# A change of engine for the duplicate of k's larger part in a three-block transformer kernel: VectorE in place of a GpSimd transfer

## The chip, the cores and the metric

The kernel runs on one core of a Trainium2 chip. The metric is the device time of one launch in microseconds; the time shown for a kernel is the median of several runs. TensorE (PE in the profile, PEld for its weight loads) multiplies matrices, VectorE (DVE) and ScalarE (ACT) work elementwise on up to 128 partitions, GpSimd (POOL) here clears tiles and issues some transfers, and SyncE (SP) issues the loads of weights. SBUF holds tiles of 128 partitions; PSUM takes TensorE's results.

## What is computed

The input x is 512 tokens of 1024 float32 values. Three blocks follow one another, each adding its result to x.

```python
def first_block(x, ...):            # block 1
    h = rms_norm(x, norm_mix)
    q, kc_raw, vc_raw, ks, vs, kw, vw, gates, hq, hf, hi, hg = split(h @ w_in)
    q, ks, kw = rms_norm of each head with its gain (ks, kw: 2 groups of 64)
    o_nsa  = gated sum of compressed, selected and windowed attention, 8 heads of 64
    o_hgrn = hgrn2_mixer(hq, hf, hi, hg)        # 4 heads of 128, chunks of 64
    x = x + concat(o_nsa, o_hgrn) @ w_out
    gate, up = split(rms_norm(x, norm_ffn) @ w_gate_up)
    return x + (silu(gate) * up) @ w_down

for l in range(2):                  # the two later layers, L0 and L1
    sb_q, sb_k, sb_v, df_q, df_k, df_v = split(rmsnorm(x) @ w_in[l])
    sb = stick_breaking_attention(sb_q, sb_k, sb_v)             # 8 heads of 64
    df = differential_attention(rope(df_q), rope(df_k), df_v)   # 4 x 2 heads of 64
    x = x + concat(sb, rmsnorm(df) * (1 - lambda_init)) @ w_o[l]
    x = x + square(relu(rmsnorm(x) @ w_ff1[l])) @ w_ff2[l]      # width 4096
return rmsnorm(x)
```

Everything has to hold float32 accuracy, while TensorE multiplies in a shorter format, fp32r. So an operand is split in two parts, a larger one (the value cast to fp32r) and a smaller one (the rest, also in fp32r), and a product is the sum of three or four products of parts.

## The kernel before

**Tiles.** Activations lie with features on the partitions and the 512 tokens along the free dimension. A dense product takes a weight tile, splits it (ScalarE casts the larger part, L284, VectorE subtracts, L285) and issues three matmuls for each 128 rows of the contraction (L289 to L291).

**The pairs for scores.** Heads have 64 features, so a tile of 128 partitions holds two heads. For a score product one matmul contracts over all 128 partitions: q is stacked as larger part on the head's own 64 partitions and smaller part on the other 64 (stacked_q, L315 to L323), and k must then have its larger part on both halves, so that one matmul gives both parts of q times the larger part of k. That is what stacked_k (L325 to L333) builds. For each of the two heads g, with r the head's own partitions and o the other 64, it clears the smaller part's tile on o (GpSimd, L329), casts the larger part on r (ScalarE, L330), subtracts for the smaller part on r (VectorE, L331) and duplicates the larger part on o (L332). A second matmul takes kl. The source t is a float32 tile of 128x512.

**Who calls it.** 18 calls, so 36 duplicates of 64x512: nk0 and nk1 in block 1 (L700; the normed tile nkn of L699), and in each later layer sk1, sk3, sk5, sk7 (L956, stick-breaking attention, from tile sb) and dk0 to dk3 (L979, differential attention, from the rotated tile rt). Their readers on TensorE are the scores s (L761, L762), z (L993, L994) and ds (L1078, L1079).

**What sets the order.** The program is written as streams that yield: dense products, HGRN heads and attention units. A driver interleaves them by a cost that each announces and by shares (ORDER1 and SHARES1 for block 1, ORDER2 and SHARES2 for a later layer). After that a scheduler places every instruction in its engine's queue by its own estimate of durations, within the limits of the buffer pools and PSUM banks (two banks of pool mm for dense products, three of pool s for scores and HGRN products). Each engine then works through its queue in that order and waits where an operand or a buffer isn't there. So a change of one instruction's engine can move others on every engine.

**HGRN head 3.** The change's surroundings in block 1 are the last of the HGRN heads. emit_hgrn makes x (hx, L426), hq (L431), hk (L435) and, after a table load and a logarithm on ScalarE, the running sum hc (L440). From hc, VectorE and ScalarE make qc, kc (L473 to L477) and the scaled qx, kx (L519 to L525), which the products hpo need (L528 to L534). Then come seven levels m = 64, 32, ..., 1: two or three VectorE operations make qr and ke (L488 to L504), four 64-column matmuls give hpl (L508), and VectorE merges the result into at (L510). The diagonal hpd (L544), the product hpv (L553 to L556) and the output follow. Dense work that can stand between: wvsw (values of the attention and gates), whg (gate of HGRN) and wout (the output product, the part over finished heads).

## Time and profile before

| | before |
|---|---|
| median of 3 runs | 2021.68 us |
| the runs | 2023.47, 2021.68, 2016.97 us |
| profiled execution: time | 2023.06 us |
| profiled execution: span from first to last instruction | 2021.3 us |
| mean granted TensorE clock | 0.995 |
| TensorE busy | 1981.6 us, 98% |
| VectorE busy | 1177.0 us, 58% |
| ScalarE busy | 878.0 us, 43% |
| GpSimd busy | 44.6 us, 2% |
| GpSimd's transfer queue | 2976 packets, 4.98 MB, 1.2% of 16 engines' span |

One execution is profiled; its rows are in microseconds from the span's start unless they say ns. A wait is the idle time of an engine ahead of an instruction, put down to what released it. An arrow a<-b names the tile written and the tiles read; L0 and L1 before a name are the later layers. An operation's duration in a timeline overlaps the next one's start a little, so a group of operations takes less than the sum of its durations; the chain of waits gives the time from one to the next.

### The profile page before, as it was taken

The page shows a single profiled execution, that of the slowest core. Times are in us where ns is not written, and L with a number is a line of the kernel's source. Part 1 is how long each engine was busy: PE and PEld are TensorE (multiplying, and loading weights), DVE is VectorE, ACT ScalarE, POOL GpSimd, SP SyncE. Part 2 cuts the span into 40 slices and gives each one's busy share as a digit, 9 for nine tenths or more (in the row PEclk, how much of TensorE's full clock was granted, in tenths as well). Part 3 has the DMA queues.
Part 4 walks back from the last instruction along what each step waited for, and adds up shares of the span by engine and source line. Part 5 has one row for each costly group of instructions (what it writes and reads, how often), then busy time and mean ns, then how long its engine had stood idle before and what let it go on. Part 6 is the DMA issues. An engine that isn't in the chain of part 4 may idle for free.

```text
span 2021.3 us, 25987 instructions
## 1 busy us (share of the span) xinstructions
PE 1981.6 (98%) x10269; PEld 1614.4 (80%) x10269; DVE 1177.0 (58%) x2032; ACT 878.0 (43%) x1420; POOL 44.6 (2%) x87
## 2 busy tenths in 40 slices
PE   8999999999999999999999999999999999999998
PEld 7888867788888878777788888887878788888887
DVE  7685876744444455657864444447466874444446
ACT  6643544522222235766542223335586653322223
POOL 0000000000000000000000000000000000000000
PEclk9999999999999999999999999999999999999999
DMA  5222200122222322212222222222212222232222
GB/s 185 69 68 89 61 13 31 63 94 94 94 94 97 98 89 84 73 48 76 68 94 94 94 94 94 95 99 89 80 51 69 64 83 94 98 100 94 94 94 73
DMA packets 50921, 168.64 MB, mean 83 GB/s; under 512 B 5808, under 2 KB 8240, under 8 KB 50800
## 3 DMA queue, kind: packets, MB, share of 16 engines
q1 hardware_dynamic: 47680, 161.93, 24.5%
q0 software_dynamic: 2976, 4.98, 1.2%
q8 instruction: 81, 1.33, 0.3%
q14 instruction: 40, 0.33, 0.1%
q10 hardware_dynamic: 144, 0.07, 0.0%
HBM read 160.14 MB, written 2.10 MB: 80 GB/s over the span
## 4 chain that ended last, share of the span: by engine, by line
PE 68%; issue 23%; DVE 4%; ACT 3%; DMA 2%; POOL 0%; SPq 0%; DVEq 0%; ACTq 0%; POOLq 0%
PE L1wf_p L291 5%; PE L1wf_p L289 5%; PE L1wf_p L290 5%; PE wgu_p L291 4%; PE wgu_p L289 4%; PE wgu_p L290 4%; PE wdn_p L289 2%; PE wdn_p L290 2%; PE wdn_p L291 2%; PE po L811 1%; PE hpl L508 1%; PE pt L792 1%; PE wout_p L289 1%; PE wout_p L290 1%; PE wout_p L291 1%
## 5 line engine op out<-in xcount | busy, mean ns | idle before, releaser
L284 ACT CAST L0wf_h<-L0wf_r 128x1024 fp32r<-128x1024 f32 x64 | 67.3, 1052 | 229.3 <-PE L0wf_p L291 224.8
L284 ACT CAST L1wf_h<-L1wf_r 128x1024 fp32r<-128x1024 f32 x60 | 63.1, 1051 | 221.0 <-PE L1wf_p L291 216.7
L291 PE MATMUL wgu_p<-h_l,wgu_h 128*128 128x512 f32 x328 | 128.8, 393 | 0.0
L289 PE MATMUL wgu_p<-h_h,wgu_h 128*128 128x512 f32 x328 | 128.7, 392 | 0.0
L290 PE MATMUL wgu_p<-h_h,wgu_l 128*128 128x512 f32 x328 | 128.6, 392 | 0.0
L284 ACT CAST wgu_h<-wgu_r 128x1024 fp32r<-128x1024 f32 x44 | 46.2, 1051 | 168.3 <-issue 65.1
L289 PE MATMUL L0wf_p<-L0u_h,L0wf_h 128*128 128x512 f32 x256 | 100.7, 393 | 0.0
L290 PE MATMUL L0wf_p<-L0u_h,L0wf_l 128*128 128x512 f32 x256 | 100.4, 392 | 0.0
L291 PE MATMUL L0wf_p<-L0u_l,L0wf_h 128*128 128x512 f32 x256 | 99.4, 393 | 0.0
L291 PE MATMUL L0wf_p<-L0m_l,L0wf_h 128*128 128x512 f32 x240 | 94.2, 393 | 0.0
L291 PE MATMUL L1wf_p<-L1m_l,L1wf_h 128*128 128x512 f32 x240 | 94.2, 393 | 0.0
L289 PE MATMUL L0wf_p<-L0m_h,L0wf_h 128*128 128x512 f32 x240 | 94.2, 392 | 0.0
L289 PE MATMUL L1wf_p<-L1m_h,L1wf_h 128*128 128x512 f32 x240 | 94.2, 392 | 0.0
L290 PE MATMUL L0wf_p<-L0m_h,L0wf_l 128*128 128x512 f32 x240 | 94.1, 392 | 0.0
L290 PE MATMUL L1wf_p<-L1m_h,L1wf_l 128*128 128x512 f32 x240 | 94.1, 392 | 0.0
L285 DVE TENSOR_TENSOR L0wf_l<-L0wf_r,L0wf_h 128x1024 fp32r<-128x1024 f32 x64 | 78.4, 1225 | 24.6 <-ACT L0wf_h L284 24.6
L289 PE MATMUL L1wf_p<-L1u_h,L1wf_h 128*128 128x512 f32 x224 | 88.1, 393 | 0.0
L290 PE MATMUL L1wf_p<-L1u_h,L1wf_l 128*128 128x512 f32 x224 | 87.9, 392 | 0.0
L285 DVE TENSOR_TENSOR L1wf_l<-L1wf_r,L1wf_h 128x1024 fp32r<-128x1024 f32 x60 | 73.5, 1225 | 23.2 <-ACT L1wf_h L284 23.2
L291 PE MATMUL L1wf_p<-L1u_l,L1wf_h 128*128 128x512 f32 x224 | 86.9, 393 | 0.0
L353 DVE TENSOR_TENSOR X<-X,L0wf_p 128x512 f32<-128x512 f32 x64 | 43.9, 687 | 67.2 <-PE L0wf_p L291 67.2
L353 DVE TENSOR_TENSOR X<-X,L1wf_p 128x512 f32<-128x512 f32 x56 | 38.5, 687 | 66.6 <-PE L1wf_p L291 66.6
(841 smaller groups left out, 5392.6 us busy)
## 6 DMA issues: line engine op xcount, KB each, us to landing
L0wf_r<-w_ff SPq DMA_DIRECT2D x64, 512.0 KB, 3.3
L1wf_r<-w_ff SPq DMA_DIRECT2D x60, 512.0 KB, 3.3
wgu_r<-w_gu SPq DMA_DIRECT2D x44, 512.0 KB, 3.3
wdn_r<-w_dn SPq DMA_DIRECT2D x22, 512.0 KB, 3.3
wns_r<-w_nsa SPq DMA_DIRECT2D x8, 512.0 KB, 3.6
wout_r<-w_out SPq DMA_DIRECT2D x8, 512.0 KB, 3.3
L0wsb_r<-w_sbqk SPq DMA_DIRECT2D x8, 512.0 KB, 3.3
L0wdf_r<-w_dfqk SPq DMA_DIRECT2D x8, 512.0 KB, 3.6
```

What stands on the lines that cost most here:

```text
L284: S.copy(hi[:, c], raw[:, c])
L285: V.tensor_tensor(lo[:, c], raw[:, c], _f(hi)[:, c], ALU.subtract)
L289: TE.matmul(ps, lh, rh, start=start, stop=False)
L290: TE.matmul(ps, ll, rh, start=False, stop=False)
L291: TE.matmul(ps, lh, rl, start=False, stop=stop)
L353: V.tensor_tensor(X[m], X[m], ps, ALU.add)
L508: TE.matmul(pl[:, b * 64 : (b + 1) * 64], ke[:, b * P : (b + 1) * P], qr[:, b * 64 : (b + 1) * 64], start=True, stop=True)
L792: TE.transpose(pt[:, o + j * P : o + (j + 1) * P], p[g][:, j * P : (j + 1) * P], ident)
L811: TE.matmul(po[g * 64 : (g + 1) * 64, 0:P], vsw[:, j, br * 128 + g * 64 : br * 128 + (g + 1) * 64], p[g][:, j * P : (j + 1) * P], start=Fa ...
```

## The change

L332, the last line of the loop in stacked_k, wrote the duplicate as a transfer from SBUF to SBUF, issued by GpSimd and reading ScalarE's result. It becomes a VectorE copy that reads the float32 source t on partitions r and writes fp32r on partitions o.

```diff
         for g, (r, o) in enumerate(((lower, upper), (upper, lower))):
             G.memset(_f(kl[o, g]), 0.0)
             S.copy(kh[r, g], t[r])
             V.tensor_tensor(kl[r, g], t[r], _f(kh[r, g]), ALU.subtract)
-            G.dma_start(kh[o, g], kh[r, g])
+            V.tensor_copy(kh[o, g], t[r])
         return kh, kl
```

All 36 transfers leave GpSimd's queue, and 36 copies (CAST in the order of instructions) come into VectorE's. The scheduler orders the engines anew. SyncE's queue changes in the place of one load only.

**VectorE, block 1, where the pairs nk0 and nk1 are made.** nkn are the normed keys of the selected and the windowed attention; hx and hq belong to HGRN head 3, wvsw_l is the smaller part of a weight. Before:

```order
L699 SCALAR_TENSOR_TENSOR nkn_1802<-nraw_712,qkg,nkpb_1793 128x512
L699 SCALAR_TENSOR_TENSOR nkn_1823<-nraw_712,qkg,nkpb_1814 128x512
L331 TENSOR_TENSOR nk0l<-nkn_1802,nk0h 64x512 x2
L331 TENSOR_TENSOR nk1l<-nkn_1823,nk1h 64x512 x2
L426 TENSOR_TENSOR hx_1888<-whqf_p_0_1863,st_rb 128x512
L285 TENSOR_TENSOR wvsw_l<-wvsw_r,wvsw_h 128x1120
L431 TENSOR_TENSOR hq_1892<-hx_1888,hsg_1890 128x512
L426 TENSOR_TENSOR hx_1925<-whqf_p_0_1900,st_rb 128x512
```

and after:

```order
L699 SCALAR_TENSOR_TENSOR nkn_1802<-nraw_712,qkg,nkpb_1793 128x512
L332 CAST nk0h<-nkn_1802 64x512 x2
L331 TENSOR_TENSOR nk0l<-nkn_1802,nk0h 64x512 x2
L699 SCALAR_TENSOR_TENSOR nkn_1823<-nraw_712,qkg,nkpb_1814 128x512
L426 TENSOR_TENSOR hx_1888<-whqf_p_0_1863,st_rb 128x512
L332 CAST nk1h<-nkn_1823 64x512
L285 TENSOR_TENSOR wvsw_l<-wvsw_r,wvsw_h 128x1120
L331 TENSOR_TENSOR nk1l<-nkn_1823,nk1h 64x512 x2
L332 CAST nk1h<-nkn_1823 64x512
L431 TENSOR_TENSOR hq_1892<-hx_1888,hsg_1890 128x512
L426 TENSOR_TENSOR hx_1925<-whqf_p_0_1900,st_rb 128x512
```

Four copies come in, and the second nkn and the nk1l pair move behind other work; hq and the second hx, with which HGRN head 3 begins, stand behind all of it.

**TensorE, block 1, the levels of HGRN head 3.** wvsw_p_2186 is the last token block of the values' product. Before, from hpl_64 on:

```order
L508 MATMUL hpl_64_1996<-qr_64_1994,kc_1951 128x64 x4
L290 MATMUL wvsw_p_2186<-wvsw_h,h_1_l 128x280
L291 MATMUL wvsw_p_2186<-wvsw_l,h_1_h 128x280
L289 MATMUL wvsw_p_2186<-wvsw_h,h_2_h 128x280
L290 MATMUL wvsw_p_2186<-wvsw_h,h_2_l 128x280
L291 MATMUL wvsw_p_2186<-wvsw_l,h_2_h 128x280
L289 MATMUL wvsw_p_2186<-wvsw_h,h_3_h 128x280
L508 MATMUL hpl_32_2009<-qr_32_2002,ke_32_2003 128x64 x4
L290 MATMUL wvsw_p_2186<-wvsw_h,h_3_l 128x280
L291 MATMUL wvsw_p_2186<-wvsw_l,h_3_h 128x280
L289 MATMUL wvsw_p_2186<-wvsw_h,h_4_h 128x280
L290 MATMUL wvsw_p_2186<-wvsw_h,h_4_l 128x280
```

and after, from the last hpo matmul on:

```order
L534 MATMUL hpo_1990<-qx_1978,kx_1979 128x256
L508 MATMUL hpl_64_1996<-qr_64_1994,kc_1951 128x64 x4
L508 MATMUL hpl_32_2009<-qr_32_2002,ke_32_2003 128x64 x4
L508 MATMUL hpl_16_2022<-qr_16_2015,ke_16_2016 128x64 x4
L508 MATMUL hpl_8_2074<-qr_8_2028,ke_8_2029 128x64 x4
L289 MATMUL wvsw_p_2186<-wvsw_h,h_0_h 128x280
L290 MATMUL wvsw_p_2186<-wvsw_h,h_0_l 128x280
L291 MATMUL wvsw_p_2186<-wvsw_l,h_0_h 128x280
```

The levels 64 to 8 stood among matmuls of wvsw and whg, and now stand together, with the wvsw block behind them.

**TensorE, a little later, at the first probabilities of the attention.** cpt are transposes of compressed-attention probabilities, pt those of the others, s scores, wout_p the output product. Before:

```order
L737 MATMUL cpt_2304<-packed,sc 128x128 x4
L737 MATMUL cpt_2309<-packed,sc 128x128 x4
L291 MATMUL wout_p_1_2662<-ho_m_l,wout_0_h 128x512
L761 MATMUL s_1_2291<-nk1h,nq_1252 128x256
L762 MATMUL s_1_2291<-nk1l,nq_1252 128x256
L763 LDWEIGHTS masks
L763 MATMUL s_1_2291<-masks 128x128
L761 MATMUL s_0_2328<-nk0h,nq_1252 128x256
L762 MATMUL s_0_2328<-nk0l,nq_1252 128x256
L763 LDWEIGHTS masks
L763 MATMUL s_0_2328<-masks 128x128
L792 MATMUL pt_0_2317<-packed,p_2277 128x128 x2
```

and after:

```order
L737 MATMUL cpt_2304<-packed,sc 128x128 x4
L737 MATMUL cpt_2309<-packed,sc 128x128 x4
L289 MATMUL wout_p_0_2542<-ho_m_h,wout_0_h 128x512
L290 MATMUL wout_p_0_2542<-ho_m_h,wout_0_l 128x512
L291 MATMUL wout_p_0_2542<-ho_m_l,wout_0_h 128x512
L289 MATMUL wout_p_0_2542<-ho_m_h,wout_0_h 128x512
L290 MATMUL wout_p_0_2542<-ho_m_h,wout_0_l 128x512
L291 MATMUL wout_p_0_2542<-ho_m_l,wout_0_h 128x512
L289 MATMUL wout_p_0_2542<-ho_m_h,wout_0_h 128x512
L290 MATMUL wout_p_0_2542<-ho_m_h,wout_0_l 128x512
L761 MATMUL s_1_2291<-nk1h,nq_1252 128x256
```

Eight of the 17 wout matmuls that stood ahead, among hpl_4 to hpv, now stand between cpt and the next scores, and the other nine a little further on.

**TensorE, first later layer, the first scores z of sk1.** L0wsb_p_0_6468 is a dense product of the stick-breaking projections. Before:

```order
L290 MATMUL L0wsb_p_0_6468<-L0h_h,L0wsb_1_l 128x512
L291 MATMUL L0wsb_p_0_6468<-L0h_l,L0wsb_1_h 128x512
L289 MATMUL L0wsb_p_0_6468<-L0h_h,L0wsb_1_h 128x512
L290 MATMUL L0wsb_p_0_6468<-L0h_h,L0wsb_1_l 128x512
L291 MATMUL L0wsb_p_0_6468<-L0h_l,L0wsb_1_h 128x512
L289 MATMUL L0wsb_p_0_6468<-L0h_h,L0wsb_1_h 128x512
L993 MATMUL L0z_6365<-L0sq_6318,L0sk1h 128x256
L994 MATMUL L0z_6365<-L0sq_6318,L0sk1l 128x256
L993 MATMUL L0z_6378<-L0sq_6318,L0sk1h 128x256
L994 MATMUL L0z_6378<-L0sq_6318,L0sk1l 128x256
```

and after:

```order
L290 MATMUL L0wsb_p_0_6468<-L0h_h,L0wsb_1_l 128x512
L291 MATMUL L0wsb_p_0_6468<-L0h_l,L0wsb_1_h 128x512
L289 MATMUL L0wsb_p_0_6468<-L0h_h,L0wsb_1_h 128x512
L993 MATMUL L0z_6365<-L0sq_6318,L0sk1h 128x256
L993 MATMUL L0z_6378<-L0sq_6318,L0sk1h 128x256
L290 MATMUL L0wsb_p_0_6468<-L0h_h,L0wsb_1_l 128x512
L291 MATMUL L0wsb_p_0_6468<-L0h_l,L0wsb_1_h 128x512
L289 MATMUL L0wsb_p_0_6468<-L0h_h,L0wsb_1_h 128x512
L290 MATMUL L0wsb_p_0_6468<-L0h_h,L0wsb_1_l 128x512
L291 MATMUL L0wsb_p_0_6468<-L0h_l,L0wsb_1_h 128x512
L994 MATMUL L0z_6365<-L0sq_6318,L0sk1l 128x256
L994 MATMUL L0z_6378<-L0sq_6318,L0sk1l 128x256
```

The first scores moved thirteen matmuls ahead, and those with the smaller part (sk1l) stand apart from them. On VectorE, the two copies for sk1h stand on either side of the split of svw_0 and the subtractions for sk1l; at sk7 the order is subtraction, copy, subtraction, copy where it was two subtractions.

## Rows read from the trace of the kernel before

**Rows 1.** The page's section 1: the span, then busy time, share of the span and number of instructions of each engine.
```profile
span 2021.3 us, 25987 instructions
...
PE 1981.6 (98%) x10269; PEld 1614.4 (80%) x10269; DVE 1177.0 (58%) x2032; ACT 878.0 (43%) x1420; POOL 44.6 (2%) x87
```

**Rows 2.** TensorE's waits over the whole span: its line and tile, what released it, us in total, times, longest.
```profile
PE L0z L993 <- DMA L0sk7h<-L0sk7h: 2.3, 1, 2.3
...
PE L1z L993 <- DMA L1sk1h<-L1sk1h: 1.5, 1, 1.5
...
PE hpo L528 <- DVE kx L521: 1.2, 2, 1.0
PE L1z L993 <- DMA L1sk7h<-L1sk7h: 1.1, 1, 1.1
PE L0z L993 <- DMA L0sk1h<-L0sk1h: 1.1, 1, 1.1
...
PE L0z L993 <- DMA L0sk3h<-L0sk3h: 0.8, 1, 0.8
...
PE L1z L993 <- DMA L1sk3h<-L1sk3h: 0.8, 1, 0.8
...
PE hpl L508 <- DVE qr L494: 0.4, 1, 0.4
```

**Rows 3.** The instructions of L332, the GpSimd transfers that the change removes: time from issue to landing.
```profile
DMA to landing us min/median/max: 2.2/2.4/4.7
```

**Rows 4.** VectorE's groups by line and shape: line, operation, tiles, out<-in shape and type, count, busy us, mean ns of one, idle time before.
```profile
L366 DVE COPY p<-pt 128x512 f32<-128x512 f32 x12 | 8.3, 689 | 8.2 <-PE pt L792 8.2
...
L778 DVE TENSOR_SCALAR p<-p,sm 128x512 f32<-128x512 f32 x16 | 7.0, 479 | 0.0
...
L488 DVE COPY qr<-qc 128x256 f32<-128x256 f32 x4 | 1.1, 284 | 0.0
```

**Rows 5.** The instructions of L330, ScalarE's cast of the larger part: duration ns min/median/max, first and last start us.
```profile
L330 ACT CAST nk0h<-nkn x2: 617/618/620, 199.3 to 200.0; 64x512 fp32r<-64x512 f32 x2
...
L330 ACT CAST L0sk1h<-L0sb x2: 613/615/617, 774.9 to 775.5; 64x512 fp32r<-64x512 f32 x2
```

**Rows 6.** The chain of waits in 196 to 250 us of block 1, in order of time: start us, us until the next piece, what.
```profile
199.40 0.75 DVE nkn L699
...
203.55 1.23 DVE wvsw_l L285
204.78 0.60 DVE hq L431
205.38 0.61 DVE hx L426
...
208.87 1.23 DVE hc L440
...
210.31 1.12 DVE cm L720
...
215.98 0.35 DVE kx L525
...
218.50 0.84 PE hpl L508 x8
```

**Rows 7.** TensorE's timeline about the first product of HGRN head 3: start us, us, line, tile, shapes, [idle before, releaser].
```profile
214.42 0.29 PE L291 MATMUL wvsw_p<-wvsw_l,h_h 128*128 128x280 f32 x1
215.70 0.49 PE L528 MATMUL hpo<-qx,kx 128*128 128x128 f32 x2 [0.99 <-DVE kx L521]
```

**Rows 8.** Stretches of 4 us in block 1: length, busy us (and instructions) of PE, PEld, DVE, ACT, POOL; then the granted TensorE clock, the DMA share, GB/s.
```profile
240.00:244.00 4.00, 3.42 (x24) 2.80 (x22) 1.67 (x10) 3.48 (x9) 0.00 (x0) 1.00 0.22 83
244.00:248.00 4.00, 2.78 (x23) 1.95 (x23) 2.29 (x11) 3.21 (x11) 0.00 (x0) 1.00 0.00 0
248.00:252.00 4.00, 4.00 (x19) 2.80 (x20) 2.11 (x11) 1.89 (x6) 0.00 (x0) 0.54 0.02 4
252.00:256.00 4.00, 4.00 (x23) 3.25 (x22) 1.89 (x6) 1.48 (x5) 0.00 (x0) 0.50 0.00 0
256.00:260.00 4.00, 4.00 (x20) 2.42 (x19) 2.65 (x12) 1.58 (x5) 0.00 (x0) 0.50 0.00 0
260.00:264.00 4.00, 4.00 (x25) 2.81 (x23) 2.24 (x9) 0.48 (x1) 0.00 (x0) 0.75 0.00 0
264.00:268.00 4.00, 2.67 (x18) 1.87 (x17) 3.71 (x15) 2.26 (x6) 0.00 (x0) 1.00 0.00 0
```

**Rows 9.** TensorE's timeline at the first scores of sk7 in the first layer; columns as in rows 7.
```profile
874.26 0.35 PE L993 MATMUL L0z<-L0sq,L0sk7h 128*128 128x256 f32 x1 [2.27 <-DMA L0sk7h<-L0sk7h]
```

**Rows 10.** VectorE's timeline at the same place.
```profile
870.02 1.40 DVE L331 TENSOR_TENSOR L0sk7l<-L0sb,L0sk7h 64x512 fp32r<-64x512 f32 x2
```

**Rows 11.** TensorE's timeline at the first scores of sk1 in the first layer.
```profile
777.55 0.39 PE L291 MATMUL L0wsb_p<-L0h_l,L0wsb_h 128*128 128x512 f32 x1
777.78 0.39 PE L289 MATMUL L0wsb_p<-L0h_h,L0wsb_h 128*128 128x512 f32 x1
778.14 0.36 PE L993 MATMUL L0z<-L0sq,L0sk1h 128*128 128x256 f32 x1
```

**Rows 12.** VectorE's timeline ahead of the pair sk1.
```profile
774.19 0.69 DVE L322 TENSOR_TENSOR L0sq<-L0sb,L0sq 64x512 fp32r<-64x512 f32 x1
```

**Rows 13.** The sum over six stretches of 8 us, 936 to 984 us, where the pairs dk1, dk2 and dk3 of the first layer are made; columns as in rows 8.
```profile
sum 48.00, PE 46.24 PEld 37.72 DVE 42.96 ACT 34.98 POOL 4.11; mean PE 7.71 PEld 6.29 DVE 7.16 ACT 5.83 POOL 0.68
```

## The prediction

> **What bounds the kernel now.** I read the page's engine line first: TensorE is busy 98% of the span, 39.7 us short of all of it, and VectorE, which receives the new work, 58% [rows 1]. So whatever the change gains or loses must pass through TensorE's idle time or its clock. The second view is the list of TensorE's waits [rows 2]: a reader should look there for the names of the pairs that the removed transfers fill. Six rows have them: 2.3, 1.5, 1.1, 1.1, 0.8 and 0.8 us, together 7.6 us, all at the first scores of three of the four stick-breaking pairs in each later layer. The other 12 pairs, all of block 1's and all of the differential attention's among them, never hold TensorE up. The third is where the transfer's time goes: 2.2 to 4.7 us from issue to landing [rows 3], against some half a microsecond for one pass of an engine over the same tile. The fourth is the clock: TensorE is granted 1.00 nearly all the way; the exception that costs is 248 to 264 us, at 0.54, 0.50, 0.50 and 0.75, which follows two stretches in which it was busy 3.42 and 2.78 of 4 us [rows 8]. In lost full-speed time these rows make 4 x (0.46 + 0.50 + 0.50 + 0.25) = 6.8 us.
>
> The change is one line, but a scheduler orders each engine's instructions, and it has reordered all four compute engines. So there are three terms: the waits removed, the work added to VectorE, and what the new order does.
>
> **The transfers removed.** 36 transfers go, and with them 36 GpSimd issues, an engine that is 2% busy: worth nothing by themselves. The new copy reads the float32 tile instead of ScalarE's result, so it needn't wait for ScalarE either.
>
> **The copies added.** 36 VectorE copies of 64x512 from float32 to float32r. The trace holds no such copy. From below, the nearest row is a single-source pass over 512 columns of SBUF, 0.479 us; the one copy from SBUF to SBUF, of 256 columns, took 0.284. From above, a 512-column copy out of PSUM took 0.689 [rows 4]. I take 0.48, because that row too has one source and both ends in SBUF; back to back an operation costs some 0.08 less (0.61 for a 0.69 one [rows 6]), so 0.40 to 0.61. In all 14 to 22 us of VectorE's time, beside 844 us in which it is idle.
>
> The Trainium skill, "VectorE: DVE Perf Modes", section "The perf-mode tier table", puts a float32 copy within SBUF at twice the rate of a two-source operation; the rows above agree for float32 results, and no row here shows one that writes float32r. By that table the copy would be at the lower end, by its one-times tier at the upper.
>
> **Where the 7.6 us go.** At sk7 of the first layer TensorE came to the pair at 872 us and stood 2.27 us [rows 9]. VectorE began the two subtractions at 870.02 [rows 10]; now it does subtraction, copy, subtraction, copy, so the halves are there at about 871.1 and 872.2. The first score has moved five matmuls of 256 columns earlier, by some 0.6 us to 871.2, and the second comes some 0.8 us later: a residue of 0.2 to 0.6 us. At sk1 the first score has moved thirteen matmuls earlier, at 0.23 us each from 778.14 to some 775.2 [rows 11]. VectorE is free for the copy from 774.9 [rows 12]; ScalarE ends its half at 775.5 [rows 5]: 0.3 us of wait there. Behind it stand the 1.2 us split of a weight, the two subtractions and only then the second copy: 0.1 to 0.5 at the low part and 0.3 to 0.6 at the second half. Together 0.7 to 1.4 us, where 1.06 stood: the faster copy is spent on an earlier place. At sk3 the wait of 0.8 goes. Twice over (the layers are alike): 1.8 to 4.0 us left of 7.6, a gain of 3.6 to 5.8; I take **-4.7**.
>
> **The differential pairs.** Between 936 and 984 us VectorE is busy 42.96 of 48 us [rows 13]. Three pairs fall there: six copies, 2.4 to 3.7 us, into 5.0 us of slack, while the residual additions that free PSUM queue behind them. That cover could hold, at no cost; if it were gone, TensorE would wait for most of the copies. I take 0.5 a layer: **+1.0**, with bounds 0 and +3.
>
> **HGRN head 3 in block 1.** This is where I expect a new wait. VectorE is saturated from 199 us on and stands on the path there: the chain of waits goes through its operations from 199.40 to the last kx at 215.98 [rows 6]. Two copies now stand behind the first nkn, and two more and the nk1l pair ahead of hq and hx. Walked by the rows: the first nkn ends at 199.3 [rows 5]; two copies 0.80, two subtractions 1.2, the second nkn 0.7, hx 0.6, copy 0.40, the weight split 1.23, two subtractions 1.2, copy 0.40, hq 0.60, hx 0.61, which makes 207.0 where it ended at 205.99: 1.0 us later, and 1.9 at the dearer copy. All of hc, kc and kx follow. The new order wins back 0.74 ahead of kx by placing one ke and one gl elsewhere, so hpo starts some 0.3 us later and TensorE idles 1.3 us instead of 0.99 [rows 7].
>
> Worse is what TensorE has beside it. Before, the levels hpl_64 to hpl_8 stood among 24 wvsw matmuls and 12 whg matmuls. Now four levels come one after the other with nothing in between. Each needs VectorE's chain, at 0.35 for a merge or a half tile, 0.60 for a full tile and 1.12 for a pass over 1024 columns [rows 6]. hpl_64 has a ke, a 1024-column pass and a copy ahead of it and waits about 0.5; hpl_32 needs merge and ke after hpl_64, 1.0; hpl_16 has a 1024-column reduction ahead of it as well, 1.5; hpl_8 0.4; the wvsw block then needs a PSUM bank that VectorE frees behind two merges and two ke, 1.2. With hpo that is 1.3 + 0.2 + 4.6 = 6.1 us of idle time, 7.0 with the dearer copy. Before, 1.2 and 0.4 us stood here [rows 2], and 0.58 + 1.22 = 1.8 us at 240 to 248 [rows 8], 3.4 in all. That later gap is now filled: the 17 wout matmuls that served as cover among hpl_4 to hpv stand behind hpv and cpt, among the first probability transposes. Net **+2.7**, up to +3.6.
>
> **The clock.** The dip at 248 follows 1.8 us of idle time in 8. If the gap there is filled, its cause is gone: -6.8. But 6.1 us of idle time in some 12, between 215 and 227, is more than what preceded the dip, so I expect one there. Its length no row gives. As long as the old one, the clock term is 0; with none it is -6.8. What follows this time are whg matmuls of 512 columns without a wait between, where scores and transposes followed the old one, so I put it below the old length, but nearer to it than to none: **-2**.
>
> **Sum.** -4.7 + 1.0 + 2.7 - 2 = -3.0 us against the profiled execution's own 2023.06 us. That execution lies 1.4 above the median; from the median 2021.68 the sum gives 2018.7 us, 0.15% faster. A measurement of this kernel tells some 0.3%, 6 us, from no change, so this forecast is "no difference".
>
> **Rivals.**
> (a) *No new dip.* The idle pieces at the hpl levels are each under 1.6 us with matmuls between, and at 872 one of 2.27 us [rows 9] brought none. Then the clock term is -6.8: -4.7 + 1.0 + 2.7 - 6.8 = -7.8, 2013.9 us, and with the good end of the waits and no cost at the differential pairs some 2012. Against it: the hpl stretch is the emptiest of the block.
> (b) *Two dips, slower.* The first comes at the hpl stretch; the clock is back by 240, so the block's softmax meets a full-speed TensorE, and the gap that stood at 264 to 268 (busy 2.67 of 4 [rows 8]), or one like it, is followed by a second. Price +6.8 instead of -2: -4.7 + 1.0 + 2.7 + 6.8 = +5.8, 2027.5. It decides from the point where a second stretch is as empty as 244 to 248. With the copy at its dearer end (1.9 us late at hx, the larger residues, the full price at the differential pairs) it is -3.6 + 3 + 3.6 + 6.8 = +9.8, 2031.5.
> (c) *Hidden anyway.* 30 of the 36 transfers (all but one half of six pairs) had no waiter, and TensorE meets the next late thing at the same places, VectorE's subtraction of the low part: the 7.6 us shrink to 2 or 3, the hpl stretch costs what it wins, and the time stays at 2021.7.
> (d) *The copy runs at the dearer end* without a second dip: -3.6 + 2 + 3.6 - 2 = 0, 2021.7. It falls in with (c).
>
> **Chances.** The forecast with (c) and (d), all within 0.3%: 0.47. (a): 0.30, nearly all of it faster by over 0.3% (below 2015.6). (b): 0.23, about the dividing line of 2027.7 or above, and with other new waits of the reordered layers I count it whole as slower. The range leaves out the best corner of (a) and the worst of (b): 2011.5 to 2029.
>
> **What would show it.** Right: no DMA among the releasers of L0z and L1z; waits of TensorE for VectorE or ScalarE at sk1 of 0.7 to 1.4 a layer; the copy at 0.42 to 0.5 us; hpl rows with VectorE as releaser making 4 to 6 us between 215 and 228; the clock at 0.50 somewhere in 218 to 245 and at 1.00 from 248 to 262. Wrong: a copy at 0.69; the clock at 1.00 through all of block 1, which is (a); two dips, which is (b); waits above 1 us at the differential scores or for PSUM banks in the later layers, which no term here has.

## The result: slower by half a per cent

| | before | after |
|---|---|---|
| median of 8 runs each | 2023.43 us | 2031.96 us |
| lowest to highest | 2016.97 to 2027.35 | 2027.40 to 2037.15 |
| ratio, with its 95% interval | | 1.0055 (1.0040 to 1.0071) |
| profiled execution, span | 2021.3 us | 2030.3 us |
| mean granted TensorE clock | 0.995 | 0.992 |

The time lies above the forecast range of 2011.5 to 2029, and the interval lies wholly on the slower side of the 0.3% that a measurement of this kernel can tell. The page's engine line of the changed kernel answers to [rows 1]:

```profile
span 2030.3 us, 25930 instructions
...
PE 1989.5 (98%) x10269; PEld 1620.1 (80%) x10269; DVE 1195.2 (59%) x2068; ACT 877.1 (43%) x1420; POOL 27.1 (1%) x51
```

The 36 operations have gone from POOL to DVE, and VectorE is busy 18.2 us more. The span is 9.0 us longer, and TensorE's busy time, with as many matmuls, is 7.9 us longer. At half the clock the matmuls of wvsw_p (280 columns) follow one another in 0.23 us instead of 0.13 and count as busy all that time, so this already says that part of the loss isn't idle time.

**The copy** was priced right. The instructions of L332 in the changed kernel (duration ns min/median/max, first and last start):

```profile
L332 DVE CAST nk0h<-nkn x2: 421/423/425, 198.3 to 198.8; 64x512 fp32r<-64x512 f32 x2
L332 DVE CAST nk1h<-nkn x2: 423/874/1326, 202.0 to 206.0; 64x512 fp32r<-64x512 f32 x2
L332 DVE CAST L0sk1h<-L0sb x2: 420/422/423, 780.1 to 783.1; 64x512 fp32r<-64x512 f32 x2
```

35 of the 36 take 0.42 us, the lower of the two bounds, though they write to the other 64 partitions. One, the first of nk1h, takes 1.33; more on it below. (The Trainium skill, "VectorE: DVE Perf Modes", section "The perf-mode tier table", puts a float32 copy within SBUF in its two-times tier, which the prediction took for the lower bound; 0.42 here agrees with that.)

**TensorE's waits**, the view of [rows 2], in the changed kernel:

```profile
PE hpo L528 <- DVE kx L521: 3.3, 2, 3.1
...
PE hpl L508 <- DVE ke L504: 1.3, 1, 1.3
PE hpl L508 <- ACT ke L500: 1.3, 1, 1.3
PE wvsw_p L289 <- DVE gl L602: 1.3, 1, 1.3
...
PE L0wo_p L289 <- ACT L0do_m_h L244: 1.0, 1, 1.0
PE L1wo_p L289 <- ACT L1do_m_h L244: 1.0, 1, 1.0
...
PE L1dpt L1103 <- DVE L1dp L1092: 0.7, 1, 0.7
PE L0dpt L1103 <- DVE L0dp L1092: 0.7, 1, 0.7
```

No DMA releases L0z or L1z any more: all six waits of the removed transfers are gone. In their place stand waits for VectorE and ScalarE at two kinds of place: HGRN head 3 in block 1 (hpo, hpl, wvsw_p) and the end of the differential attention in each later layer (dpt, wo_p).

**Where the time went, by stretch.** The first or last start of a tile's matmuls marks off the same work in both traces. Block 1's attention and HGRN run here from the last wns_p to the first wgu_p; a later layer's stick-breaking part up to the last dvw_p (with the feed-forward part ahead of it), its differential part from there to the last wo_p. The column after_again is a second profiled execution of the changed kernel, from a later set of runs (see below). The marks are read to 0.1 us.

| stretch | before, us | after | after_again | forecast |
|---|---|---|---|---|
| block 1, wns_p to wgu_p | 219.7 | +6.1 | +9.1 | +0.7 |
| L0 up to dvw_p | 509.8 | -2.9 | -3.2 | -2.35 |
| L0, dvw_p to wo_p | 113.0 | +5.0 | +3.7 | +0.5 |
| L1 up to dvw_p | 512.7 | -2.9 | -2.9 | -2.35 |
| L1, dvw_p to wo_p | 113.1 | +4.8 | +3.6 | +0.5 |

The gain is there and somewhat larger than forecast, -5.8 against -4.7. Block 1 and the differential parts together lose nearly three times as much.

**Block 1.** TensorE's timeline of the changed kernel about HGRN head 3 (columns as in [rows 7]):

```profile
218.34 0.55 PE L528 MATMUL hpo<-qx,kx 128*128 128x128 f32 x2 [3.10 <-DVE kx L521]
...
223.94 1.08 PE L508 MATMUL hpl<-qr,ke 128*128 128x64 f32 x8 [1.28 <-ACT ke L500]
226.34 3.64 PE L508 MATMUL hpl<-qr,ke 128*128 128x64 f32 x16 [1.32 <-DVE ke L504]
231.25 0.60 PE L289 MATMUL wvsw_p<-wvsw_h,h_h 128*128 128x280 f32 x1 [1.27 <-DVE gl L602]
```

That is 6.97 us of idle time where [rows 7] has 0.99 for hpo. Over 196 to 400 us TensorE's idle rows sum to 12.15 us, against 7.58 before: +4.6. And the clock fell in the same place. Stretches of 4 us in the changed kernel, columns as in [rows 8]:

```profile
200.00:204.00 4.00, 4.00 (x35) 3.84 (x33) 3.90 (x5) 2.89 (x4) 1.50 (x3) 1.00 0.00 0
204.00:208.00 4.00, 4.00 (x23) 4.00 (x23) 3.94 (x8) 0.00 (x0) 0.00 (x0) 0.62 0.42 131
...
216.00:220.00 4.00, 1.53 (x4) 1.13 (x5) 4.00 (x13) 2.65 (x6) 0.00 (x0) 0.83 0.01 2
220.00:224.00 4.00, 2.72 (x14) 2.35 (x12) 3.06 (x7) 3.23 (x7) 0.00 (x0) 0.74 0.00 0
224.00:228.00 4.00, 2.68 (x16) 2.58 (x17) 3.33 (x7) 0.57 (x1) 0.00 (x0) 0.68 0.00 0
228.00:232.00 4.00, 2.73 (x13) 2.54 (x13) 2.97 (x8) 2.10 (x4) 0.00 (x0) 0.50 0.00 0
232.00:236.00 4.00, 4.00 (x20) 4.00 (x19) 2.18 (x6) 0.92 (x3) 0.00 (x0) 0.50 0.00 0
236.00:240.00 4.00, 4.00 (x24) 4.00 (x24) 1.65 (x4) 0.97 (x1) 0.00 (x0) 0.61 0.01 4
```

The seventh column is the granted clock; 0.50 is the lower of its two levels, 1.2 GHz. It falls where TensorE is busy 1.53 and about 2.7 of 4 us, stays low through 228 to 236 and is back by 240. From 248 to 252, where the kernel before stood at 0.54 [rows 8], it is 1.00. So the dip moved, as forecast, and grew: in lost full-speed time the six stretches from 216 make 4 x (0.17 + 0.26 + 0.32 + 0.50 + 0.50 + 0.39) = 8.6 us, against 6.8 before. The dip at 205 to 208.4 us, another 1.7, is of another kind: TensorE is busy 4.00 of 4 us ahead of it and has no wait in the 30 us before, so the new waits don't explain it.

**Differential attention.** TensorE's timeline at the end of the first layer's wo product, changed kernel:

```profile
1014.61 0.50 PE L289 MATMUL L0wo_p<-L0do_m_h,L0wo_h 128*128 128x512 f32 x1 [1.03 <-ACT L0do_m_h L244]
...
1016.83 0.50 PE L289 MATMUL L0wo_p<-L0do_m_h,L0wo_h 128*128 128x512 f32 x1 [0.55 <-DVE X L353]
```

Neither wait exists before. Idle rows of this part sum to 4.66 us against 2.62.

### The profile page after: what moved, and what is told of

The parts are those of the page before. It is cut to its first block, busy times and chain, and to the rows that moved or that the text cites. A ratio compares the mean times of both kernels' runs of the same rounds, so it can differ in the third digit from the quotient of the medians.

```text
span 2030.3 us, 25930 instructions
## 1 busy us (share of the span) xinstructions
PE 1989.5 (98%) x10269; PEld 1620.1 (80%) x10269; DVE 1195.2 (59%) x2068; ACT 877.1 (43%) x1420; POOL 27.1 (1%) x51
## 3 DMA queue, kind: packets, MB, share of 16 engines
q8 instruction: 81, 1.33, 0.3%
## 4 chain that ended last, share of the span: by engine, by line
PE 90%; ACT 4%; DVE 4%; issue 1%; DMA 0%; SPq 0%; DVEq 0%; ACTq 0%
PE L0wf_p L291 6%; PE L0wf_p L289 6%; PE L0wf_p L290 6%; PE L1wf_p L291 5%; PE L1wf_p L289 5%; PE L1wf_p L290 5%; PE wgu_p L291 4%; PE wgu_p L289 4%; PE wgu_p L290 4%; PE wdn_p L289 2%; PE wdn_p L290 2%; PE wdn_p L291 2%; PE hpl L508 1%; PE po L811 1%; PE pt L792 1%
```

## The experiments

The theory to be tested: each group of pairs acts by itself. The block-1 pairs (nk) cost, by the new order and by VectorE's chain there; the stick-breaking pairs (sk) win what the waits cost; the differential pairs (dk) cost, because VectorE has no slack there. The rivals in turn: that the clock alone makes the difference, that it is the copy's work and not the order, that it is VectorE and not the end of the transfers that matters.

All edits are of L332, by the name of the pair; S.copy is the same copy on ScalarE. The first three are the parts of the change.

### nk_only: the copy for block 1's pairs alone

```diff
-            G.dma_start(kh[o, g], kh[r, g])
+            V.tensor_copy(kh[o, g], t[r]) if "nk" in name else G.dma_start(kh[o, g], kh[r, g])
```

> Only the four copies of nk0 and nk1 in block 1 go to VectorE; the pairs of the later layers keep the transfer. Theory (order and place): block 1 gets the whole new order of the changed kernel and with it the loss of some 6 us between the first score pair and the output product that the changed kernel's landmarks show (+6.1); the later layers stay as before. So about +6 us (0.3%), with a dip of the clock ahead of the HGRN head-3 levels. Rival (VectorE's added time): the loss goes with the number of copies; 4 of 36 copies would cost some 1 us, no measurable change.

Measured: 2027.92 us (10 runs) against 2021.52 (21), ratio 1.0032 (1.0018 to 1.0046). Its block 1 has the changed kernel's order and its later layers that of before. TensorE's longest waits, then the clock's stretches, in this run:

```profile
PE hpo L528 <- DVE kx L521: 2.7, 2, 2.6
PE hpl L508 <- DVE ke L504: 2.5, 2, 1.3
...
PE wvsw_p L289 <- DVE gl L602: 1.3, 1, 1.3
```

```profile
216.00:220.00 4.00, 2.83 (x8) 2.33 (x9) 4.00 (x10) 2.35 (x5) 0.00 (x0) 0.60 0.00 0
220.00:224.00 4.00, 2.72 (x13) 2.50 (x13) 2.62 (x6) 3.10 (x6) 0.00 (x0) 0.50 0.00 0
224.00:228.00 4.00, 2.79 (x14) 2.63 (x14) 2.70 (x6) 0.00 (x0) 0.00 (x0) 0.50 0.00 0
```

The same waits as in the changed kernel, a little shorter, and the same fall of the clock, which lasts from 216.8 to 244.1 us here. Four copies, 2.6 us of VectorE's time with the stretched one among them, cost 6.4 us, where the rival had some 1.

### sk_only: the copy for the stick-breaking pairs alone

```diff
-            G.dma_start(kh[o, g], kh[r, g])
+            V.tensor_copy(kh[o, g], t[r]) if "sk" in name else G.dma_start(kh[o, g], kh[r, g])
```

> Only the 16 copies of sk1 to sk7 in the two later layers go to VectorE. Theory (order and place): these are the only pairs whose transfer TensorE waited for, and the stretch has VectorE time to spare, so the gain of 2.8 to 3.0 us a layer stays alone: -5 to -6 us, the only one of the three that is faster than before. Rival (VectorE's added time): 16 of 36 copies cost 16/36 of what the change lost on top of the waits, some 15 x 0.44 = +6.6 against -5.8: about no change.

Measured: 2011.50 us (6 runs) against 2021.52, ratio 0.9956 (0.9939 to 0.9973): the lowest ratio of this study. VectorE at sk7 of the first layer, where [rows 10] has two subtractions, and TensorE at the score that waited 2.27 us [rows 9]:

```profile
865.41 0.68 DVE L331 TENSOR_TENSOR L0sk7l<-L0sb,L0sk7h 64x512 fp32r<-64x512 f32 x1
866.11 0.42 DVE L332 CAST L0sk7h<-L0sb 64x512 fp32r<-64x512 f32 x1
866.56 0.69 DVE L331 TENSOR_TENSOR L0sk7l<-L0sb,L0sk7h 64x512 fp32r<-64x512 f32 x1
867.28 0.42 DVE L332 CAST L0sk7h<-L0sb 64x512 fp32r<-64x512 f32 x1
```

```profile
866.97 0.39 PE L993 MATMUL L0z<-L0sq,L0sk7h 128*128 128x256 f32 x1 [0.15 <-ACT L0e L1031]
```

The first copy ends at 866.53; the score starts at 866.97, and what it waits for is ScalarE's tile for the earlier unit, for 0.15 us. The second ends at 867.70, and the next score starts at 867.91. By the marks of the first table the later layers' stick-breaking parts are 6.2 us shorter than before, which agrees with the changed kernel's 5.8. The rest of the 10 us goes with the clock: its mean makes 6.4 us of lost time a run against 11.5 (how this is worked out stands with the table at the end). Up to the pair sk1 of the first layer the order of all four engines is that of before. Behind it only the dips that follow the wait at sk7 can go with the change: 1.7 us of lost time, in two of the six profiled executions that have this wait. So the change explains little of this gain, and of the ratio some 6 us are the change's.

### dk_only: the copy for the differential pairs alone

```diff
-            G.dma_start(kh[o, g], kh[r, g])
+            V.tensor_copy(kh[o, g], t[r]) if "dk" in name else G.dma_start(kh[o, g], kh[r, g])
```

> Only the 16 copies of dk0 to dk3 in the two later layers go to VectorE. Theory (order and place): no wait was there to remove, VectorE is nearly full when dk1 to dk3 are made, and the last head's probabilities come later: +4.5 to +5 us a layer, +9 to +10 us, a third of it from a new dip of the clock in each layer. Rival (VectorE's added time): as many copies as sk_only, so the same loss of some 6.6 us; or, if the loss is in block 1 alone, no change.

Measured: 2028.01 us (12 runs) against 2021.52, ratio 1.0033 (1.0017 to 1.0050). The size is 3 us short of what was expected, since the clock doesn't fall in the differential parts here, and it is the rival's number (+6.6). What speaks against the rival, by which the copies cost by their count, is sk_only: as many copies, and faster. The two differential parts are 3.6 and 3.4 us longer, and both waits at wo_p are there:

```profile
1011.44 0.50 PE L289 MATMUL L0wo_p<-L0do_m_h,L0wo_h 128*128 128x512 f32 x1 [1.03 <-ACT L0do_m_h L244]
1013.64 0.50 PE L289 MATMUL L0wo_p<-L0do_m_h,L0wo_h 128*128 128x512 f32 x1 [0.54 <-DVE X L353]
```

How it comes: before, 90 matmuls of wo were left as cover behind the last product of the attention's normalisation (do_pb at 1005.16); here 80 are left behind the same product at 1009.35. Eight microseconds about the last attention unit, before and here (columns as in [rows 8]):

```profile
968.00:976.00 8.00, 6.87 (x37) 5.25 (x36) 7.76 (x16) 5.09 (x12) 0.00 (x0) 1.00 0.20 66
```

```profile
966.00:974.00 8.00, 6.54 (x33) 4.61 (x32) 7.87 (x20) 6.84 (x16) 0.00 (x0) 1.00 0.21 67
```

VectorE, the third engine in the row, is busy 7.76 and 7.87 of 8 us, with six copies more in its queue here, so the last attention unit comes later while TensorE has gone on with wo, and what should have covered that unit's end is used up. Of the 3.5 us a layer 2.0 are idle rows; the rest is in no wait that the profile shows.

### dk_act: the same copies on ScalarE

```diff
-            G.dma_start(kh[o, g], kh[r, g])
+            S.copy(kh[o, g], t[r]) if "dk" in name else G.dma_start(kh[o, g], kh[r, g])
```

> The 16 copies of dk0 to dk3 go to ScalarE instead (0.62 us each), all other pairs keep the transfer. Theory (in dk_only the six copies of dk1 to dk3 lengthen VectorE's queue, which paces the last attention units): ScalarE is busy 34.98 of 48 us there, VectorE 42.96, so the loss of +5.6 us goes to 0 to +2. Rival (any engine's copy, by the order that it brings, delays the last unit): +5 or more, as with VectorE.

Measured: 2014.65 us (12 runs) against 2017.44 (35), ratio 0.9992 (0.9979 to 1.0004). The waits at wo_p are gone, the differential parts' idle rows sum to 2.8 us a layer as before, and the parts are 0.9 and 0.7 us longer. So it is VectorE's queue, or the order that comes with it, that made the dk pairs cost, not the missing transfers. An unexpected gain came with it: the new order also took away the waits at sk7 in both layers (2.27 and 1.07 us before), whose transfers are still there, and the stick-breaking parts are 5.3 us shorter. The waits for the transfers of sk1 and sk3 stay, 0.84 to 1.37 us each.

### sk_act: the stick-breaking copies on ScalarE

```diff
-            G.dma_start(kh[o, g], kh[r, g])
+            S.copy(kh[o, g], t[r]) if "sk" in name else G.dma_start(kh[o, g], kh[r, g])
```

> The 16 copies of sk1 to sk7 go to ScalarE. Theory (the 2.2 to 4.7 us of the transfer are what TensorE waited for): any engine's copy of 0.4 to 0.6 us takes the waits away, so -4 to -6 us, close to sk_only. Rival (it has to be VectorE, because ScalarE's exponentials of the stick-breaking units queue behind the copies): half the gain or less, -3 to +1 us.

Measured: 2014.26 us (12 runs) against 2017.44, ratio 0.9972 (0.9958 to 0.9987). Each copy takes 0.62 us there, and the stick-breaking parts are 8.3 us shorter: no score waits for a transfer any more, whichever engine writes the duplicate. The theory holds at sk1 and sk3; at sk7, as dk_act shows, a new order can take the wait away as well, and what the copy alone does there is not separated.

### nk0_only and nk1_dk0: which of block 1's pairs

```diff
-            G.dma_start(kh[o, g], kh[r, g])
+            V.tensor_copy(kh[o, g], t[r]) if "nk0" in name else G.dma_start(kh[o, g], kh[r, g])
```

> Only the two copies of nk0 go to VectorE. TensorE's order then keeps hpl_64 to hpl_16 among the wvsw matmuls, as before, and only moves the wout matmuls from ahead of hpv to the first probability transposes. Theory (the cover of the HGRN levels makes the loss): no loss; the gap at 243 to 248 us is filled, so idle time falls by 0 to 1.5 us and the clock's dip there gets shorter or goes: -1 to -6 us. Rival (two more copies in a full stretch of VectorE): half of what both pairs cost, +3 us.

Measured: 2023.32 us (12 runs) against 2017.44, ratio 1.0026 (1.0011 to 1.0041). The theory fell: with the levels' cover in place I had expected a gain. The cover is not whole: one level waits 1.79 us for its ke (0.41 before). But the largest wait has another cause, as VectorE's timeline in this run, then TensorE's, show:

```profile
206.04 0.68 DVE L426 TENSOR_TENSOR hx<-whqf_p,st_rb 128x512 f32<-128x512 f32 x1
209.16 0.29 DVE L712 TENSOR_TENSOR sc<-cs,packed 128x128 f32<-128x128 f32 x1 [2.44 <-PE cs L709]
...
212.60 0.68 DVE L426 TENSOR_TENSOR hx<-whqf_p,st_rb 128x512 f32<-128x512 f32 x1
```

```profile
223.73 0.79 PE L528 MATMUL hpo<-qx,kx 128*128 128x128 f32 x2 [3.94 <-DVE kx L521]
```

The scheduler put sc, which needs a product that isn't there, at the head of VectorE's queue. VectorE stands 2.44 us, the second hx with all that hangs on it comes at 212.60, and hpo waits 3.94 us. The two copies themselves take 0.84.

```diff
-            G.dma_start(kh[o, g], kh[r, g])
+            V.tensor_copy(kh[o, g], t[r]) if "nk1" in name or "dk0" in name else G.dma_start(kh[o, g], kh[r, g])
```

> The copies of nk1 and of dk0 (2 + 4 of 36) go to VectorE; TensorE's order is that of the kernel before, to the instruction, and VectorE's differs only about the copies. Theory (place and order): nk1's copies delay hx by up to 0.9 us, so the wait before hpo grows from 0.99 to at most 2 us, and the levels keep their cover; dk0 is made where VectorE has room and costs nothing: 0 to +1 us. Rival (VectorE's added time): half of nk_only and a quarter of dk_only, 3.2 + 1.6 = +4.8 us.

Measured: 2023.06 us (12 runs) against 2017.44, ratio 1.0015 (0.9999 to 1.0030). Here TensorE's order is that of before, instruction for instruction, and the idle rows of 196 to 285 us sum to 4.64 us against 4.60: no cost in waits, as the theory has it, though the wait stands ahead of wvsw_p (1.27) and not of hpo. The time is inconclusive: the interval holds the theory's 0 to +1 us and the rival's +4.8, and of a mean of 3.5 us more, 3.1 are lost clock.

### nk_act: block 1's copies on ScalarE

```diff
-            G.dma_start(kh[o, g], kh[r, g])
+            S.copy(kh[o, g], t[r]) if "nk" in name else G.dma_start(kh[o, g], kh[r, g])
```

> The four copies of nk0 and nk1 on ScalarE, the later layers by the transfer. TensorE's order is that of the kernel before, to the instruction; ScalarE has 2.5 us more ahead of hsg, and VectorE's split of wvsw stands behind two additions that wait for TensorE. Theory (the cover of the HGRN levels decides): idle time grows ahead of hpo by 0 to 2 us and nowhere else: 0 to +2 us. Rival (a late hx costs the same whatever the order, because all levels follow it): +3 us or more.

Measured: 2024.90 us (12 runs) against 2018.82 (29), ratio 1.0024 (1.0012 to 1.0035). TensorE's order is again that of before, and its idle rows sum to 6.31 us against 4.60 (hpo 2.06, and against the theory also wvsw_p 0.88). Here too sc stands at the head of VectorE's queue, for 2.21 us, so hx is late. The theory is right on the size of the idle time, +1.7, the rival on the time; of a mean of 3.7 us more, 1.8 are lost clock. So block 1's duplicates are best left with the transfer, which nobody waits for.

### sk_v_dk_a and sk_a_dk_a: do the gains add?

```diff
-            G.dma_start(kh[o, g], kh[r, g])
+            V.tensor_copy(kh[o, g], t[r]) if "sk" in name else S.copy(kh[o, g], t[r]) if "dk" in name else G.dma_start(kh[o, g], kh[r, g])
```

> The copies of sk1 to sk7 on VectorE, those of dk0 to dk3 on ScalarE, nk0 and nk1 by the transfer as before. Theory (each copy belongs on the engine with room at its place, and block 1 is left alone): the gains add, -6 to -8 us, a version faster than both kernels. Rival (the scheduler's order decides, and a new combination is a new order): anything from -8 to +5 us, with new waits in the lists that neither sk_only nor dk_act has.

```diff
-            G.dma_start(kh[o, g], kh[r, g])
+            G.dma_start(kh[o, g], kh[r, g]) if "nk" in name else S.copy(kh[o, g], t[r])
```

> All 32 copies of the two later layers on ScalarE, nk0 and nk1 by the transfer. Theory (the transfer's latency was what TensorE waited for, and ScalarE has room in both stretches): -6 to -9 us, like the sum of sk_act and dk_act. Rival (32 x 0.62 = 20 us more on ScalarE crowd out the exponentials): the gain of sk_act is given back, -2 to +2 us.

Measured: 2016.30 us (12 runs) against 2018.82, ratio 0.9987 (0.9972 to 1.0001), and 2011.98 us (12 runs), ratio 0.9967 (0.9953 to 0.9982). The first missed what I expected: the stick-breaking parts are 6.5 us shorter, as in sk_only, and the dk copies add 1.7 in the differential parts; 3.0 of the 5.3 that dk_act won by its order are waits at sk7 that the copies take away too, so they can't be won twice. The second came out as expected, and near sk_only (0.9967 against 0.9956, intervals overlapping).

### sk_port: a GpSimd operation that reads beside the copies

The slow copy of nk1h (1.33 us) lies beside GpSimd's clearing of tiles. POOL and VectorE in the changed kernel:

```profile
201.51 1.09 POOL L329 MEMSET nk1l<- 64x512 f32 x2 [45.63 <-DVE nkn L699]
202.55 0.52 POOL L479 MEMSET at<- 128x512 f32 x1
```

```profile
202.03 1.33 DVE L332 CAST nk1h<-nkn 64x512 fp32r<-64x512 f32 x1
```

The copy begins while GpSimd is in its MEMSETs and ends at 203.36, 0.29 us after the last of them. In nk_only it is the same (1.33 us), and in nk1_dk0 a copy that starts later in the MEMSET takes 1.07. This run puts a GpSimd operation beside the stick-breaking copies:

```diff
-            G.memset(_f(kl[o, g]), 0.0)
+            G.tensor_scalar(kl[o, g], t[o], 0.0, None, ALU.mult) if "sk" in name else G.memset(_f(kl[o, g]), 0.0)
...
-            G.dma_start(kh[o, g], kh[r, g])
+            V.tensor_copy(kh[o, g], t[r]) if "sk" in name else G.dma_start(kh[o, g], kh[r, g])
```

> As sk_only, but GpSimd writes the zeros of the smaller part's tile for sk1 to sk7 as a multiple (0) of the source tile, so that it starts when the copy can start instead of long before. In the changed kernel one copy of nk1 took 1.33 us beside a clearing by GpSimd, and 35 took 0.42. Theory (the copy runs at two elements a cycle only while GpSimd leaves the port free): copies that overlap a GpSimd operation take 0.8 us or more, the two-source subtractions keep 0.68. Rival (the long copy of nk1 had another cause, its place in the queue): all copies keep 0.42.

Measured: 2015.01 us in one run, against 2011.50 for sk_only; the stick-breaking parts are 2.1 us shorter than before instead of 6.2. POOL and VectorE at sk1 and sk5 of the first layer:

```profile
766.77 3.92 POOL L329 TENSOR_SCALAR L0sk1l<-L0sb 64x512 fp32r<-64x512 f32 x2 [25.54 <-DVE L0sb L955]
776.50 3.49 POOL L329 TENSOR_SCALAR L0sk5l<-L0sb 64x512 fp32r<-64x512 f32 x2 [5.81 <-DVE L0sb L955]
```

```profile
769.36 0.74 DVE L332 CAST L0sk1h<-L0sb 64x512 fp32r<-64x512 f32 x1
...
776.78 0.61 DVE L332 CAST L0sk5h<-L0sb 64x512 fp32r<-64x512 f32 x1
...
778.68 0.98 DVE L322 TENSOR_TENSOR L0sq<-L0sb,L0sq 64x512 fp32r<-64x512 f32 x1
```

Theory and rival both fell in part. The four copies that begin while the operation runs take 0.60 to 0.74 us instead of 0.42, so they are slowed, but none is held to the operation's end; four that begin just ahead of it keep 0.42. And two-source operations are slowed too: 8 of the 15 of 64x512 that begin beside it take 0.98 to 1.11 us instead of 0.68. The Trainium skill, "SBUF — State Buffer", section "Who interferes with whom", says that such a copy and GpSimd exclude each other for a whole instruction, and that a two-source operation contends with a GpSimd operation that reads. The copy beside the MEMSET and the slower subtractions agree with it; the copies of 0.60 to 0.74, within GpSimd operations of 1.5 to 2.0 us, do not show the whole exclusion (spans of POOL are rough).

### after_again: the changed kernel once more

No edit: a second set of runs, with a prior expectation of where the clock falls.

> The changed kernel once more, for a second profile and a second set of runs beside the kernel before on one chip. Its first profile had dips of the clock at 205, 219 and 225 to 239 us of block 1 and one of 3.4 us in each later layer. Theory (the emptied stretch at the HGRN levels brings the dip there, the others come and go from run to run): half speed within 215 to 245 us again, for 10 us or more; the dips at 205 us and in the later layers may be missing; the time is +8 to +12 us. Rival (all five dips belong to the new order): the same five again.

Measured: 2032.52 us (7 runs) against 2017.85 (12), ratio 1.0054 (1.0033 to 1.0075). Same waits again (hpo 3.08, hpl 1.27 and 1.21, wvsw_p 1.27; the differential idle rows 4.67), and the clock:

```profile
220.00:224.00 4.00, 1.26 (x3) 1.00 (x4) 4.00 (x13) 2.25 (x6) 0.00 (x0) 0.72 0.01 4
224.00:228.00 4.00, 3.52 (x14) 3.01 (x12) 2.61 (x6) 3.25 (x6) 0.00 (x0) 0.50 0.00 0
...
232.00:236.00 4.00, 3.58 (x16) 3.39 (x16) 2.33 (x7) 0.94 (x2) 0.00 (x0) 0.50 0.00 0
236.00:240.00 4.00, 3.15 (x14) 3.15 (x15) 3.33 (x9) 2.00 (x4) 0.00 (x0) 0.50 0.00 0
```

The lower level holds from 221.8 to 242.3 us, in the same emptied stretch. So the clock falls again for well over 10 us within 215 to 245: the theory holds, and the rival falls. Two more dips stand at 191 to 198 and 208 to 211.5 us, with TensorE busy without a wait for 30 us before each. In this execution no dip stands in the later layers, and the differential parts are 3.7 and 3.6 us longer, as in dk_only: the 1.3 more of the first trace go with a dip of 3.4 us in each part.

### All runs side by side

Lost clock is the span times one minus the mean granted clock, averaged over the runs of a kernel, minus the same for the kernel before beside it (for after, whose neighbours have no clock on record, minus the four such means of the other sets of runs); from the scatter of the runs it is good to 1 to 2 us. The middle columns are from one profiled execution each, against that of before, by the marks of the first table.

| kernel | ratio | block 1 | both stick-breaking parts | both differential parts | lost clock |
|---|---|---|---|---|---|
| after | 1.0055 | +6.1 | -5.8 | +9.8 | +5.5 to +7.4 |
| after_again | 1.0054 | +9.1 | -6.1 | +7.3 | +6.9 |
| nk_only | 1.0032 | +8.1 | +0.3 | +0.2 | +4.3 |
| sk_only | 0.9956 | -3.4 | -6.2 | +0.4 | -5.2 |
| dk_only | 1.0033 | +1.8 | -1.5 | +7.0 | +0.4 |
| nk0_only | 1.0026 | +4.9 | +0.3 | +0.1 | +1.7 |
| nk1_dk0 | 1.0015 | +2.7 | -1.8 | +0.3 | +3.1 |
| nk_act | 1.0024 | +3.6 | -1.6 | +0.1 | +1.8 |
| dk_act | 0.9992 | -3.9 | -5.3 | +1.6 | -1.2 |
| sk_act | 0.9972 | +4.7 | -8.3 | 0.0 | +2.2 |
| sk_v_dk_a | 0.9987 | -5.2 | -6.5 | +1.7 | +0.6 |
| sk_a_dk_a | 0.9967 | -5.9 | -8.2 | +1.8 | -2.1 |
| sk_port | one run | -5.3 | -2.1 | 0.0 | |

The differential column repeats within 0.5 us among like kernels (the dips of after apart), the stick-breaking column within some 2 (nk_act and nk1_dk0, with TensorE's order of before throughout, have -1.6 and -1.8). The block-1 column doesn't repeat: the kernels whose sk or dk pairs alone are changed leave TensorE's order in block 1 as it was, and yet it ranges from -5.9 to +4.7, because the dips there come and go between executions. A single trace can't size them; the means over runs can. By these, the changed kernel loses 17.0 us a run to the clock (8 runs; 16.5 in after_again), and the kernel before 9.6 to 11.5. The difference of 5.5 to 7.4 us lies above what the kernels with an unchanged order in block 1 show (-5.2 to +3.1), though not by much.

The place of the dips says more. Between 212 and 270 us lie the HGRN levels and the first probabilities. In dips that begin there the lower level holds 17.1, 20.5 and 27.3 us in the three profiled executions with the changed kernel's order of TensorE in block 1 (after, after_again, nk_only), each time within 215 to 245. In the ten with the order of before it holds 0 to 17.1 us, 8.5 in the mean, and within 215 to 245 only nk_act has any (3.4, behind its wait of 2.06 at hpo). nk0_only, with an order of its own, has 10.2. Half of the difference, 6.5 us, is the lost time, which agrees with the means.

## Why the prediction was wrong, point by point

- **The removed waits: right.** -4.7 forecast, -5.8 measured in the span, and no DMA among the releasers. The residue of 0.7 to 1.4 us at sk1 was too cautious: no such wait stands in the list, neither at the high nor at the low part. So rival (c), by which the next late thing would take the place of the transfers, is out too.
- **The copy: right,** at its lower bound, 0.42 us. So rival (d) is out. Not foreseen was the one copy that GpSimd's MEMSET stretched by 0.9 us, and it is on the path: by the walk of the prediction hx is late by about 1 us without it, and by 0.9 more with it.
- **HGRN head 3: right in kind, short in size.** 6.1 us of idle time was forecast for hpo, the levels and wvsw_p; 6.97 stand there (hpo 3.1 instead of 1.3, the levels 2.6 instead of 3.4). The net over block 1 is +4.6 rather than +2.7. The walk itself was short: from the end of the first nkn to the end of hx it has 7.7 us, and the trace of the changed kernel 9.5. The stretched copy makes 0.9 of the difference; half of the rest comes from the four subtractions, which take 0.70 us each, as two of them do in [rows 10], and not the 0.60 of the walk. Another part of hpo's excess comes from a queue that I did not walk, ScalarE's; its timeline in the changed kernel:

```profile
209.11 0.47 ACT L601 ACTIVATE vsw<-wvsw_p,st_rn 128x256 f32<-128x256 f32 x1 [5.20 <-PE wvsw_p L291]
209.48 0.62 ACT L428 ACTIVATE hsg<-hx 128x512 f32<-128x512 f32 x1
```

vsw now stands ahead of hsg and waits for a product, so hsg starts at 209.48 although VectorE's hx was there at 207.76. The dip of the clock at 205 makes it worse here, and so does the one at 208 in after_again, where hsg is as late; without one, in nk_only, hsg starts 0.19 us behind hx, and hpo waits 2.55.
- **The clock: the step that failed.** The prediction had a dip at the right place, 218 to 245, none at 248, and took -2 because it held the old length, 13.7 us, for the upper end. The runs show +5.5 to +7.4: with the new order the lower level holds 17.1 to 27.3 us there. And the old dip was no fixed price: with the order of before it lasts 0 to 17.1 us, so even where it goes, 4.3 us are won in the mean and not 6.8. Rival (a) had argued that the wait of 2.27 us at 872 us brought no dip; in nk_only and nk0_only one of 3.4 us follows the like wait at sk7 (1.56 and 2.06 us). Rival (b) had the sign and nearly the price, +6.8, but by a second dip behind a gap at 264 to 268; what came is one longer stretch, or several short ones, at the emptied levels, while TensorE is busy two thirds to nine tenths of the time and is served at half speed.
- **The differential pairs: the other step that failed,** with +1.0 and bounds of 0 and +3. It measured +7.0 (dk_only) and +7.3 (after_again). The prediction counted the copies' own time against VectorE's slack [rows 13]. What decides is the cover: TensorE runs ahead through wo while the last attention unit comes later. It shows as waits of wo_p for do_m_h and X, which no term of the prediction has; its last sentence names only waits at the differential scores and for PSUM banks. dk_act shows that VectorE is the engine; whether it is its longer queue or the order that follows from it is not separated.

With the measured terms the sum is -5.8 + 7.0 + 4.6 + 6 = +11.8 us, against +11.1 from the ratio (0.0055 x 2023), 8.5 between the medians and 9.0 between the profiled spans. By its parts measured alone it is nk +6.4, sk -10, dk +6.5, together +2.9: short of the whole by 8 us. Some 5 of these are sk_only's luck with the clock; for the rest, a few us, the scatter of the clock in three separate measurements is enough, and no run settles it.

## What to carry to other kernels

A long transfer that nobody waits for is not worth replacing: here 30 of 36 had no waiter, and the 20 of block 1 and of the differential attention, replaced, cost 13 us (6.4 and 6.5), twice the 6 us that the others gave. So change the engine by place: the copy for the stick-breaking pairs alone is faster, by some 6 us. An engine's mean load (58%) says little: ask for the load of the stretch, and how much work of the next engine remains as cover when the added work has pushed its chain back. And where a scheduler sets the order, walk every engine's queue for an instruction that now waits at its head, as sc did on VectorE and vsw on ScalarE.

## What the runs showed of the hardware

- A VectorE copy of 64x512 from float32 to fp32r, onto the other 64 partitions, takes 0.42 us; the same on ScalarE 0.62.
- Beside a GpSimd MEMSET it takes 1.07 to 1.33 us and ends 0.3 us after the last one (four executions of three kernels); when it begins beside a GpSimd TENSOR_SCALAR, 0.60 to 0.74 (sk_port, one execution).
- In 97 runs of the kernel before, beside the experiments, the mean granted clock lay anywhere from 0.990 to 0.998 and the time from 2014.5 to 2029.7 us, with nothing changed. Half a per cent has to be measured in many runs, and the clock's part read from their mean.
- In nine of the fourteen profiled executions the clock falls to 0.50 once or twice between 190 and 215 us, for 3.4 or 6.8 us at a time, with no wait of TensorE in the 30 us before. No run shows what brings these dips; they come with the old order and with the new.
